# A subtraction on GpSimd exchanged for an activation and an accumulating DMA, in a kernel that splits its weights in two

## The chip, the cores and the metric

The kernel runs on one core of one Trainium2 chip. The metric is the time of one execution on the device in microseconds (us); lower is better. The engines are named as in the profile: PE is TensorE, DVE is VectorE, ACT is ScalarE, POOL is GpSimd, SP is SyncE.

## What is computed

Two transformer blocks follow each other over 256 tokens of width 1024. The first has three kinds of attention (differential, forgetting and chunked), a gated MLP with a short convolution, and a per-layer embedding. The second has two layers: an mLSTM with stick-breaking attention, then a gated delta rule, each followed by cross attention to a memory of 256 rows and by a squared-ReLU MLP. Nearly all of the arithmetic is in products with weight matrices:

```python
def reference(x, p, ln_mix, w_in, ...):
    x = first_block(x, p, ln_mix, w_in, ...)
    return second_block(x, mem_2, mix_norm_2, ab_w_in_2, ...)

def second_block(x, mem, ...):
    memn = rmsnorm(mem, mem_norm)
    for l in range(DEPTH_2):
        h = rmsnorm(x, mix_norm[l])
        if l % 2 == 0:
            x = x + ab_mixer(h, ...)
        else:
            x = x + c_mixer(h, ...)
        x = x + mem_cross_attn(rmsnorm(x, xa_norm[l]), memn, ...)
        x = x + sq_relu_mlp(rmsnorm(x, mlp_norm[l]), mlp_w1[l], mlp_w2[l])
    return rmsnorm(x, final_norm)
```

All tensors are float32.

## The kernel before, in words

The weights lie in HBM as one array `w` of 188 chunks, each 128 partitions by 2048 floats (1 MB), in the order in which they are used. TensorE is fed with fp32r operands, and the accuracy of float32 is kept by splitting each operand x in two: `hi` is x rounded to fp32r, `lo` is the rest, x - hi. A product is then three matmuls (hi by hi, hi by lo, lo by hi), so a chunk costs PE 48 matmuls of 256 columns.

`fetch` (line 436) loads and splits a chunk. It takes two halves of 1024 columns one after the other. For each, a DMA on SP's queue brings the half into a tile `raw` (line 448, four buffers), ACT writes `hi` as a rounded copy of it (line 452), and a tensor_tensor writes `lo` = raw - hi (line 454). That subtraction runs on DVE for most halves. The table `W["pool"]` (line 21) says for each chunk whether POOL does the second half (1), both (2) or none (0); there are 67 such halves, the two first of them of 512 columns (the very first chunk is loaded in quarters), the others of 1024. The names `lo`, `hi` and `raw` in the rows are these tiles. `hi` and `lo` have three buffers each.

`chunk` (line 463) is called when PE's program comes to a chunk; it makes sure that this chunk and the two after it have been fetched. The new chunk's `hi` and `lo` therefore wait for the matmuls of the chunk three before, and PE needs them two chunks later. `gemm_ab` (line 470) and `gemm_c` (line 498) issue the 48 matmuls of a chunk; in `gemm_ab` the second half is first read in the middle of the chunk, in `gemm_c` at its fourth matmul, unless it is called with `mid`.

Between the matmuls `pump` lets the other tasks issue their steps: the attentions, the convolutions and the delta rule. PE's instructions stay in the order of the program. On DVE, ACT, POOL and SP the order is laid down when the program is built, by a scheduler that plays the program through on a clock of its own; each engine then runs its list strictly in that order, and an instruction that waits holds up all behind it. So the change can move instructions which it does not name.

The stage from 803 to 964 us is `c_mixer` (the delta rule). Here DVE runs convolutions in float32 (tiles `Vm`, six scalar_tensor_tensor per chunk, line 375), products with decays (`X`), and a serial solve of small triangular blocks in `base` (tiles `t` and `I`, lines 1554 and 1556) whose result goes through HBM (`di`, `ci`) to the `solve` steps. At the start of the program (0 to 20 us) `norm` makes the first operand while chunk 0 is loaded in quarters; the statistics `R` and `rc` are written by ACT (`rstd`, line 555), and ACT's `V` needs `rc`.

Of the kernel before, what the change touches and what calls it, by code (L numbers as in the profile page):

```python
# [8 lines left out]
F32 = mybir.dt.float32  # L9
F32R = mybir.dt.float32r  # L10
AF = mybir.ActivationFunctionType
ALU = mybir.AluOpType
# [252 lines left out]
class Prog:  # L265
# [170 lines left out]
    def fetch(self, i, between=None):  # L436

        if i in self.cache or i >= len(CH):
            return
        hi = self.ring.tile([128, 2048], F32R, tag="hi", name="hi")  # L440
        lo = self.ring.tile([128, 2048], F32R, tag="lo", name="lo")
        for n in range(2):
            raw = self.ring.tile([128, 1024], F32, tag="raw", name="raw", bufs=4)
            for q in range(2 if between else 1):
                w = 512 if between else 1024
                s = slice(1024 * n + w * q, 1024 * n + w * q + w)
                r = raw[:, w * q:w * q + w]
                self.lastload = self.nc.sync.dma_start(r, self.io["w"][i, :, s]).ins.name
                if between:
                    between(2 * n + q)  # L450
                pl = n >= 2 - W["pool"][min(i, len(W["pool"]) - 1)]
                a = self.act(hi[:, s], r, AF.Copy)
                self.lastcast = a.ins.name
                d = self.tt(lo[:, s], r, hi[:, s].bitcast(F32), ALU.subtract, self.nc.gpsimd if pl else None)
                if self.after:
                    self.order(a, self.after[0])
                    if not pl:
                        self.order(d, self.after[1])
        self.after = None
        k = 8 if CH[i][2] == "A" else 2  # L460
        self.cache[i] = hi.rearrange("p (k c) -> p k c", k=k), lo.rearrange("p (k c) -> p k c", k=k)
# [1313 lines left out]
```

## Time and profile before

| | us |
|---|---|
| median of three runs | 1338.04 |
| lowest and highest of them | 1329.89, 1340.52 |
| the profiled execution | 1327.06 |
| its span, first to last instruction | 1325.3 |

The profile is of one execution, a little below the lowest of the three runs. In it PE is busy for 95% of the span, DVE for 70%, ACT for 55% and POOL for 21%; the mean granted clock of PE is 0.986. In the rows, "busy" is the time in which an engine had an instruction in execution, and the bracket behind a row is the time for which its engine was idle before it and what ended that wait.

### The profile page before, as it was taken

To read this page: it belongs to the slowest core of one execution; us is meant where nothing else is said; L and a number is where in the kernel's file an instruction comes from. 1 tells how busy PE (TensorE), PEld (TensorE's weight loads), DVE (VectorE), ACT (ScalarE), POOL (GpSimd) and SP (SyncE) were. 2 spreads that over 40 slices of the span, in tenths; PEclk is the share of its full clock that TensorE was granted. 3 is DMA by queue.
4 is the path that set the end of the run, shared out by engine and by line. 5 is a ranking of instruction groups with operands and counts; after the bars stand their busy time and mean duration, and the time that the engine had idled before them with its cause. 6 is when DMAs were issued, how large, how long until landed. Compare 5 with 4: busy or idle time off the path is not lost. (4 is left out here: it accounts for less than half of the span.)

```text
span 1325.3 us, 24944 instructions
## 1 busy us (share of the span) xinstructions
PE 1261.3 (95%) x10195; PEld 1220.8 (92%) x10195; DVE 922.0 (70%) x1401; ACT 727.8 (55%) x1217; POOL 276.1 (21%) x160
## 2 busy tenths in 40 slices
PE   8899999999999999989999999888899989999997
PEld 8788889999999999989999998878799989999997
DVE  6777678777887664786656657988685385865564
ACT  6665475655486554655444446554553564644442
POOL 4500330000224200262000015434204271100000
PEclk8999989999999999999999999999999999999999
DMA  8433455555566544444655555433334343456551
GB/s 271 137 106 106 140 163 178 177 190 192 176 212 198 186 145 144 149 136 141 206 189 182 185 184 171 134 92 119 95 108 136 111 145 128 161 189 191 187 185 43
DMA packets 65698, 208.40 MB, mean 157 GB/s; under 512 B 13192, under 2 KB 14752, under 8 KB 65584
## 3 DMA queue, kind: packets, MB, share of 16 engines
q1 hardware_dynamic: 56976, 200.76, 46.4%
q0 software_dynamic: 1600, 4.88, 1.2%
q10 hardware_dynamic: 7008, 1.18, 0.5%
q8 instruction: 80, 1.31, 0.4%
q14 instruction: 34, 0.28, 0.1%
HBM read 205.32 MB, written 1.44 MB: 156 GB/s over the span
## 5 line engine op out<-in xcount | busy, mean ns | idle before, releaser
L355 ACT ACTIVATE hi<-raw 128x1024 fp32r<-128x1024 f32 (+1 forms) x378 | 378.7, 1047 | 223.1 <-issue 98.2
L372 DVE TENSOR_TENSOR lo<-raw,hi 128x1024 fp32r<-128x1024 f32 (+1 forms) x311 | 378.5, 1251 | 164.6 <-ACT hi L355 164.1
L381 PE MATMUL pg<-oh,hi 128*128 128x256 f32 x1632 | 467.0, 286 | 7.1 <-DVE K L372 2.7
L381 PE MATMUL pg<-ol,hi 128*128 128x256 f32 x1632 | 459.3, 281 | 4.6 <-DVE ol L375 4.0
L381 PE MATMUL pg<-oh,lo 128*128 128x256 f32 x1632 | 457.5, 280 | 0.0
L381 PEld LDWEIGHTS pg<-oh,hi 128*128 128x128 f32 x1632 | 308.5, 189 | 11.9 <-issue 3.4
L381 PEld LDWEIGHTS pg<-ol,hi 128*128 128x128 f32 x1632 | 308.0, 189 | 9.9 <-DVE ol L375 8.5
L381 PEld LDWEIGHTS pg<-oh,lo 128*128 128x128 f32 x1632 | 308.7, 189 | 0.0
L372 POOL TENSOR_TENSOR lo<-raw,hi 128x1024 fp32r<-128x1024 f32 (+1 forms) x67 | 170.9, 2564 | 630.8 <-ACT hi L355 613.8
L381 PE MATMUL acc<-mh,hi 128*128 128x256 f32 x688 | 193.4, 281 | 0.7 <-ACT mh L355 0.7
L381 PE MATMUL acc<-mh,lo 128*128 128x256 f32 x688 | 193.3, 281 | 0.0
L381 PE MATMUL acc<-mlo,hi 128*128 128x256 f32 x512 | 143.9, 281 | 0.0
L381 PEld LDWEIGHTS acc<-mh,lo 128*128 128x128 f32 x688 | 131.9, 192 | 0.0
L381 PEld LDWEIGHTS acc<-mh,hi 128*128 128x128 f32 x688 | 129.2, 188 | 1.0 <-ACT mh L355 0.9
L381 PE MATMUL pg<-hi,oh 128*128 128x256 f32 x352 | 105.0, 298 | 6.2 <-DVE u L372 3.6
L381 PE MATMUL pg<-lo,oh 128*128 128x256 f32 x352 | 101.1, 287 | 1.1 <-DVE lo L372 1.1
L381 PE MATMUL pg<-hi,ol 128*128 128x256 f32 x352 | 100.8, 286 | 0.0
L381 PEld LDWEIGHTS acc<-mlo,hi 128*128 128x128 f32 x512 | 96.1, 188 | 0.0
L381 PE MATMUL acc<-oh,hi 128*128 128x256 f32 x320 | 91.8, 287 | 0.5 <-ACT oh L355 0.5
L381 PE MATMUL acc<-ol,hi 128*128 128x256 f32 x320 | 90.5, 283 | 0.0
L381 PE MATMUL acc<-oh,lo 128*128 128x256 f32 x320 | 90.2, 282 | 0.0
L372 POOL TENSOR_TENSOR sq<-sq 128x512 f32<-128x512 f32 (+1 forms) x20 | 27.5, 1375 | 255.9 <-ACT sq L355 254.6
(382 smaller groups left out, 1917.0 us busy)
## 6 DMA issues: line engine op xcount, KB each, us to landing
raw<-in_w SPq DMA_DIRECT2D x374, 512.0 KB, 4.4
mt<-in_memT POOLq DMA_DIRECT2D x12, 256.0 KB, 3.7
h<-in_xT SPq DMA_DIRECT2D x4, 256.0 KB, 4.6
raw<-in_w SPq DMA_DIRECT2D x4, 256.0 KB, 5.1
fl<-in_rel SPq DMA_DIRECT2D x3, 256.0 KB, 5.8
gw<-in_gw POOLq DMA_DIRECT2D x2, 256.0 KB, 3.2
out<-h SPq DMA_DIRECT2D x2, 256.0 KB, 2.7
con<-in_con SPq DMA_DIRECT2D x1, 384.0 KB, 8.2
```

Source lines behind the costliest of these rows:

```text
L355: return self.nc.scalar.activation(out, in_, func, **k)
L372: return (eng or self.nc.vector).tensor_tensor(out, a, b, op)
L381: i = self.nc.tensor.matmul(out, lhsT=l, rhs=r, start=start, stop=stop, skip_group_check=True)
```

## The change

For the halves that the table gives to POOL, ACT writes the negated copy of `raw` into `lo`, rounded like `hi`, right behind the copy into `hi`; then a DMA issued by POOL reads the same half of the weights from HBM once more and adds it onto `lo`. In the end `lo` is again w - hi. The table is unchanged, and so are the other halves.

```diff
                 pl = n >= 2 - W["pool"][min(i, len(W["pool"]) - 1)]
                 a = self.act(hi[:, s], r, AF.Copy)
                 self.lastcast = a.ins.name
-                d = self.tt(lo[:, s], r, hi[:, s].bitcast(F32), ALU.subtract, self.nc.gpsimd if pl else None)
+                if pl:
+
+                    self.act(lo[:, s], r, AF.Copy, scale=-1.0)
+                    self.nc.gpsimd.dma_start(lo[:, s], self.io["w"][i, :, s], accum_op=ALU.add)
+                else:
+                    d = self.tt(lo[:, s], r, hi[:, s].bitcast(F32), ALU.subtract)
                 if self.after:
```

PE's list is the same, instruction for instruction. The others differ as follows, besides the exchange itself.

ACT at the start, before. `R` and `rc` are the statistics of the first norm, `hi` of 1024 columns belong to chunks 1 and 2, `con`, `blkr` and `gwp` are constants and gate weights:

```order
L355 ACTIVATE hi<-raw 128x512
L355 ACTIVATE sq<-h 128x512 x2
L355 ACTIVATE hi<-raw 128x1024 x2
L359 ACTIVATE R<-ps_278,eps 128x256
L359 ACTIVATE rc<-ps_278,eps 128x2
L355 ACTIVATE hi<-raw 128x1024
L359 ACTIVATE R<-R 128x256
L359 ACTIVATE rc<-rc 128x2
L355 ACTIVATE hi<-raw 128x1024
L355 ACTIVATE blkr<-con_182 128x128
L355 ACTIVATE V<-pg,rc 128x256 x2
```

The same place now:

```order
L355 ACTIVATE hi<-raw 128x512
L355 ACTIVATE lo<-raw 128x512
L355 ACTIVATE sq<-h 128x512 x2
L355 ACTIVATE hi<-raw 128x1024 x4
L355 ACTIVATE blkr<-con_184 128x128
L355 ACTIVATE gwp<-gw 128x8x64
L355 ACTIVATE con_198<-raw 128x512
L359 ACTIVATE R<-ps_280,eps 128x256
L359 ACTIVATE rc<-ps_280,eps 128x2
L355 ACTIVATE hi<-raw 128x1024
L359 ACTIVATE R<-R 128x256
L359 ACTIVATE rc<-rc 128x2
```

The negated copy came in behind `hi`, and `R` and `rc` moved behind the casts of `gwp` and `con`, for whose DMAs ACT waits.

ACT in the middle of `c_mixer`, before, at about 894 to 911 us of the profile (`K` and `u` are steps of the convolution, `ssq` small evictions):

```order
L355 ACTIVATE hi<-raw 128x1024 x2
L355 ACTIVATE ssq<-ps_10394 128x4
L359 ACTIVATE K<-Vm 128x512
L355 ACTIVATE u<-K 128x512
L355 ACTIVATE Vm<-u,cols 128x256 x2
L355 ACTIVATE hi<-raw 128x1024 x2
L355 ACTIVATE ssq<-ps_10472 128x4
L359 ACTIVATE K<-Vm 128x512
```

The same place now:

```order
L355 ACTIVATE hi<-raw 128x1024 x2
L355 ACTIVATE lo<-raw 128x1024
L355 ACTIVATE Vm<-u,cols 128x256 x2
L355 ACTIVATE ssq<-ps_10438 128x4
L359 ACTIVATE K<-Vm 128x512
L355 ACTIVATE hi<-raw 128x1024 x2
L355 ACTIVATE u<-K 128x512
L355 ACTIVATE lo<-raw 128x1024 x2
L355 ACTIVATE Vm<-u,cols 128x256 x2
```

One or two negated copies stand in front of each pair of `Vm`, and `u` now follows a pair of `hi`.

POOL in the second layer's mixer, before:

```order
L372 TENSOR_TENSOR sq<-sq 128x512 x2
L372 TENSOR_TENSOR u<-sq 128x256
L517 DMA gw<-in_gw 128x512
L1046 DMA mt<-in_memT 128x512 x2
L372 TENSOR_TENSOR lo<-raw,hi 128x1024 x2
L1046 DMA mt<-in_memT 128x512
L372 TENSOR_TENSOR lo<-raw,hi 128x1024 x19
L1046 DMA mt<-in_memT 128x512
```

And now:

```order
L372 TENSOR_TENSOR sq<-sq 128x512
L457 DMA lo<-in_w 128x1024
L372 TENSOR_TENSOR sq<-sq 128x512
L372 TENSOR_TENSOR u<-sq 128x256
L522 DMA gw<-in_gw 128x512
L1051 DMA mt<-in_memT 128x512 x2
L457 DMA lo<-in_w 128x1024
L1051 DMA mt<-in_memT 128x512
L457 DMA lo<-in_w 128x1024 x19
L1051 DMA mt<-in_memT 128x512
```

From here to the end of the stage POOL computes nothing; it only issues DMAs.

## Rows read from the trace of the kernel before

**Rows 1.** The page's first part: busy time of each engine.

```profile
PE 1261.3 (95%) x10195; PEld 1220.8 (92%) x10195; DVE 922.0 (70%) x1401; ACT 727.8 (55%) x1217; POOL 276.1 (21%) x160
```

**Rows 2.** Busy time by stage: stage, its length, engines (instructions), clock, DMA share, GB/s.

```profile
0.00:62.00 62.00, 52.09 (x365) 48.62 (x365) 47.54 (x91) 41.51 (x77) 33.72 (x27) 0.94 0.64 210
...
200.00:346.00 146.00, 144.71 (x1225) 144.34 (x1225) 114.36 (x179) 83.60 (x127) 0.00 (x0) 1.00 0.56 185
...
803.00:860.00 57.00, 50.32 (x391) 47.75 (x389) 50.84 (x69) 35.79 (x60) 30.68 (x16) 0.97 0.47 149
860.00:964.00 104.00, 88.58 (x626) 78.16 (x625) 83.91 (x170) 59.26 (x118) 31.96 (x12) 0.97 0.33 100
...
1062.00:1140.00 78.00, 71.87 (x581) 69.11 (x580) 58.76 (x74) 45.86 (x82) 32.99 (x19) 1.00 0.39 125
```

**Rows 3.** The same, instructions on tile lo alone: PE, PEld, DVE, POOL.

```profile
803.00:860.00 57.00, 31.38 (x110) 21.19 (x109) 7.11 (x5) 24.83 (x9) 0.97 0.47 149
860.00:964.00 104.00, 37.39 (x130) 25.73 (x130) 7.20 (x6) 31.96 (x12) 0.97 0.33 100
```

**Rows 4.** The page's costliest groups: ACT's hi and POOL's lo.

```profile
L355 ACT ACTIVATE hi<-raw 128x1024 fp32r<-128x1024 f32 (+1 forms) x378 | 378.7, 1047 | 223.1 <-issue 98.2
...
L372 POOL TENSOR_TENSOR lo<-raw,hi 128x1024 fp32r<-128x1024 f32 (+1 forms) x67 | 170.9, 2564 | 630.8 <-ACT hi L355 613.8
```

**Rows 5.** Timeline of DVE, 895 to 920 us: start, duration, instruction.

```profile
897.14 0.18 DVE L372 TENSOR_TENSOR t<-I,N 64x25 f32<-64x25 f32 x1
897.25 0.47 DVE L375 SCALAR_TENSOR_TENSOR Vm<-u,cols,Vm 128x253 f32<-128x253 f32 x1
```

**Rows 6.** Timeline of POOL in the same stretch.

```profile
903.08 6.00 POOL L372 TENSOR_TENSOR lo<-raw,hi 128x1024 fp32r<-128x1024 f32 x2 [3.09 <-ACT hi L355]
912.15 5.08 POOL L372 TENSOR_TENSOR lo<-raw,hi 128x1024 fp32r<-128x1024 f32 x2 [3.07 <-ACT hi L355]
```

**Rows 7.** The chain that ended last, 885 to 920 us: start, share, what.

```profile
897.83 2.21 DVE t L372
...
912.57 4.94 DVE Vm L375 x2
```

**Rows 8.** Timeline around chunk 113 (w2 of layer 0): ACT, then PE.

```profile
751.19 2.01 ACT L355 ACTIVATE hi<-raw 128x1024 fp32r<-128x1024 f32 x2 [3.65 <-issue]
753.10 0.58 ACT L355 ACTIVATE r<-pg 128x512 f32<-128x512 f32 x1
...
762.95 0.28 PE L381 MATMUL acc<-mh,lo 128*128 128x256 f32 x1
```

**Rows 9.** DMA queues and issues (KB each, us to landing); POOL's issuing time by line.

```profile
q1 hardware_dynamic: 56976, 200.76, 46.4%
...
raw<-in_w SPq DMA_DIRECT2D x374, 512.0 KB, 4.4
mt<-in_memT POOLq DMA_DIRECT2D x12, 256.0 KB, 3.7
...
con<-in_con SPq DMA_DIRECT2D x1, 384.0 KB, 8.2
...
L1046 POOL DMA_DIRECT2D mt<-in_memT x12 | 6.5, 546 | 27.5 <-DVE ol L375 22.9 <-DVE u L372 3.2 <-DVE oh L372 0.8
```

**Rows 10.** Timeline of ACT and POOL at the start, 3 to 48 us.

```profile
11.71 0.63 ACT L355 ACTIVATE hi<-raw 128x512 fp32r<-128x512 f32 x1 [1.05 <-DMA raw<-in_w]
...
18.80 0.48 ACT L359 ACTIVATE R<-ps,eps 128x256 f32<-128x256 f32 x1 [2.94 <-DVE lo L372]
...
23.05 0.64 ACT L355 ACTIVATE con<-raw 128x512 fp32r<-128x512 f32 x1
...
12.42 1.42 POOL L372 TENSOR_TENSOR lo<-raw,hi 128x512 fp32r<-128x512 f32 x1 [1.19 <-ACT hi L355]
```

**Rows 11.** Timeline of DVE and PE, 57 to 63 us.

```profile
58.49 3.39 DVE L375 SCALAR_TENSOR_TENSOR E<-E,s 128x128 f32<-128x128 f32 x2
...
62.53 0.80 PE L381 MATMUL ps<-w,blkr 128*128 128x512 f32 x1 [4.77 <-DVE w L372]
```

## The prediction, made before the changed kernel was run

> **What bounds the kernel now.** I began with the busy times [rows 1]: PE is in execution for 1261.3 of 1325.3 us, so whatever the other engines do, at most 64 us of pauses can be won, and only where PE pauses. The table by stage [rows 2] shows where. In the MLP from 200 to 346 us PE rests 1.3 us in 146: work on DVE, ACT or POOL is free there as long as it is in time. From 803 to 860 us PE rests 57 - 50.3 = 6.7 us, from 860 to 964 us 15.4, from 0 to 62 us 9.9, from 1062 to 1140 us 6.1; the other 26 us lie scattered. In the two stages of `c_mixer` DVE is the fullest after PE: 50.8 of 57 us (89%) and 83.9 of 104 (81%), against 63% and 57% for ACT.
>
> Much of that DVE time is no work. On a quiet DVE a `t` product takes 0.18 us and a `Vm` step 0.47 us [rows 5]. On the chain that ended last, a `t` takes 2.21 us and two `Vm` take 4.94 us [rows 7]; POOL is just then subtracting a `lo`, in the second case from 912.15 to 917.23 us [rows 6]. A DVE instruction that starts beside POOL's subtraction stands until POOL is through. That is 2.21 - 0.18 = 2.0 us for one half and (4.94 - 0.94) / 2 = 2.0 us for each of the others, close to the 2.56 us that a subtraction lasts [rows 4]. Between 895 and 920 us POOL subtracts five halves, and the chain shows four such pieces, of which the first and the last stand in the rows: some 10 us of the chain are POOL's doing.
>
> **The change, part by part.**
>
> *67 subtractions leave POOL.* Their 170.9 us [rows 4] cost nothing in themselves; what they cost is DVE's stalls, and of those only what reaches PE. Stage by stage: 860 to 964 us has 12 of the halves [rows 3]; five of them hold the chain for 10 us, and PE has 15.4 us to give back. Behind the stalls the next thing is the serial `t`/`I` solve itself and its way through HBM, which stay. I take 10. From 803 to 860 us there are 9 halves, 18 us of stalls at the same price, but only 6.7 us of pauses, and ACT rises there from 35.8 us by 9 x 1.05 to 45.2 of 57; I take 3. From 0 to 62 us a pair of short `E` steps lasts 3.39 us, and PE then waits 4.77 us for what DVE does next [rows 11]. Some 2.5 us of this go, and as much for the half before it; ACT's two copies in front of an eviction take some back: 3. From 1062 to 1140 us, where POOL goes on subtracting `kk` and `vv` and so still stalls DVE, 2 of 6.1. All other stages together: 4. Sum: 22 us.
>
> *67 copies come to ACT.* The nearest row is its own rounding copy of the same shape, 1047 ns [rows 4]: 65 x 1.05 and two of half the size, 69 us, ACT from 728 to 797 us (60%). They stand directly in front of evictions and activations that DVE or PE await. They are hidden where ACT waits for DVE anyway; at their worst they cost 69 us, at best nothing. In the MLP stages PE needs nothing sooner than before, so a microsecond of ACT is free. In `c_mixer` the copies fall into waits which DVE's stalls made, and these shrink together. I have already counted that against the 3 us of the stage 803 to 860, and add 2 us for everything else.
>
> *67 DMAs come to POOL's queue.* Issuing costs POOL 0.55 us by its own DMAs [rows 9], in place of 2.56, so what is queued behind on POOL comes earlier, once ACT's copy is done. No accumulating DMA is in this trace. From below its landing is bounded by the 3.7 us of half the size from the same queue, from above by the slowest load here, 8.2 us for 384 KB, scaled to 512 KB: 10.9. The nearest row is the plain load of the same 512 KB, 4.4 us; as it must read its destination too, I take 6. It adds 34.6 MB of reads: a load of 0.52 MB holds 16 DMA engines for 0.464 x 1325 / 200.76 x 0.52 = 1.6 us [rows 9], 67 of them 8% of the span, twice that if the destination counts like a source. From a share of 0.33 to 0.47 in `c_mixer` [rows 2] there is room for it.
>
> Is 6 us in time? In a stage where PE never pauses, chunk 113 is the measure [rows 8]: ACT ends `hi` at 753.20 and `r` at 753.68 us, the negated copy would end at 754.73, and PE reads the half at 762.95. So 8.2 us remain. At 6 us it is hidden by PE's work on the two chunks before; every microsecond over 8.2 stops PE by as much, in about 12 chunks (those of POOL's that lie where PE does not pause).
>
> The Trainium skill ("Collectives: The Full Stack", "The bandwidth ceiling: the fold count and why AG ≠ RS ≠ AR") says that a reduce in the DMA path is slower not for its addition but because it reads two sources through one ring, at about half the rate of a copy. No run here shows it; as an estimate from it the landing would be 4.4 + 1.6 = 6.0 us, and the sum stays as it is.
>
> *The first chunk.* Here nothing lies in front as cover. POOL ends its second quarter at 13.84 us [rows 10]. Now ACT's `hi` ends at 12.34, the negated copy of 512 columns at 12.9 to 13.0, and a DMA of 256 KB lands 3.7 us after its issue [rows 9], at 16.7: 3 us later, with PE waiting, since this `lo` ends the first chunk. In the new order ACT's `R` also stands behind the cast of `con`, which ran at 23.05 us where `R` ran at 18.80 [rows 10], so that the `V` behind it comes some 4 us later and holds a PSUM bank. Both push the same PE work: 4 us in all, between 0 and 7.
>
> **Sum.** -22 + 2 + 4 = -16 us. The profiled execution took 1327.06 us (span 1325.3 and 1.8 around it) and would take 1311. The median of the runs is 1338.04, 11 us above the profile; taken from that, 1322 us, or 1.2% less. About 1% is what a measurement of this kernel tells from no change.
>
> **Rivals.**
>
> *The accumulating DMA is late (slower).* Place: the chunks with 8.2 us to spare. At the upper bound of 10.9 us, 12 chunks x 2.7 = 32 us, twice the net gain: 1338 - 16 + 32 = 1354 us. It decides from about 9.5 us on, where 12 x 1.3 is the 16 us gained. For it: nothing in the trace does this operation, and the reads go to engines that are busy half of the time. Against it: the median 4.4 us is far away. Chance 0.17.
>
> For this rival the Trainium skill has a rule too ("SBUF — State Buffer", "SBUF: two separate sides"): DMAs from GpSimd's queue have their descriptors written by its cores, and a fast-mode copy on VectorE locks them out. The 12 issues of `mt` here took 546 ns on the mean and landed in 3.7 us, which shows no such wait; the rule alone would lengthen landings by less than a microsecond beside DVE's short steps.
>
> *ACT takes DVE's place (no change).* The copies stand in the same alternation of DVE and ACT that the stalls stretched. If a quarter of the 69 us of copies lies on it, 17 us, instead of the 2 that I count, the gain is gone: 1338 - 22 + 17 + 4 = 1337 us. For it: ACT would fill 45 of 57 us from 803 to 860. Against it: around 895 to 920 us ACT waits for DVE, not the reverse. Chance 0.29.
>
> *All of DVE's stalls come back.* If PE wins 80% of its 38 us of pauses in the four stages named and the start costs nothing: 30 us, 1308. Against it: `kk`, `vv` and the way through HBM remain. Chance 0.08.
>
> **How the numbers follow.** The forecast has the remaining 0.46; its own range, gains of 8 to 24 us, is 1314 to 1330. The range for the time reaches from 1302, just below the third rival, to 1352, almost the whole of the first. Faster by over 1% (below 1325): the third rival and most of the forecast, 0.08 + 0.39 = 0.47. Slower by over 1% (above 1351): the first rival and a little of the second, where ACT costs more than its price above, 0.17 + 0.03 = 0.20. Within 1%: 0.33.
>
> **What would show it.** In the profile after: POOL busy for some 140 us, 67 issues on L457 of about 0.55 us, landing near 6 us; DVE busy for some 60 to 70 us less, no `t` or `Vm` of over 1 us from 860 to 920 us; ACT at 797 us; PE's pauses from 860 to 964 us down from 15 to about 5 us; the end of chunk 0 about 3 us later. I am wrong if PE waits for `lo` from a DMA in the MLP stages, if landings lie above 9 us, or if DVE idles behind ACT's `lo` in `c_mixer` for as long as it stood behind POOL.

## The result, and the profile after

The changed kernel takes 1365.8 us (median of 4 runs, 1363.6 to 1373.5) against 1336.9 us before (now of 4 runs, too): a ratio of 1.024, 95% interval 1.021 to 1.028. It is slower by 29 us; the forecast was 1322 us and the range ended at 1352. The profiled execution took 1366.05 us, its span 1364.2.

The page's first part, its DMA queues, the group of POOL's issues and the landings (line, KB each, median us), of the changed kernel:

```profile
PE 1279.9 (94%) x10195; PEld 1240.9 (91%) x10195; DVE 847.0 (62%) x1401; ACT 789.5 (58%) x1284; POOL 158.5 (12%) x160
...
q1 hardware_dynamic: 56976, 200.76, 45.0%
q0 software_dynamic: 11248, 39.48, 14.5%
...
L457 POOL DMA_DIRECT2D lo<-in_w x67 | 58.3, 878 | 744.2 <-ACT lo L355 538.5
...
raw<-in_w SPq DMA_DIRECT2D x374, 512.0 KB, 4.8
lo<-in_w POOLq DMA_DIRECT2D x65, 512.0 KB, 9.8
...
lo<-in_w POOLq DMA_DIRECT2D x2, 256.0 KB, 7.4
```

Beside [rows 1], DVE is busy 75 us less and ACT 62 us more, about as announced. What was not announced stands in the last rows: an accumulating DMA keeps POOL for 0.88 us and lands 9.8 us after its issue, where the sum had taken 0.55 and 6. Nor was it announced that PE is busy 18.6 us longer for the same 10195 matmuls: of the 38.9 us between the two spans (1364.2 and 1325.3) only 20.3 are pauses of PE. The other half is its clock, which was granted at 0.964 on the mean, against 0.986. Busy time by stage, columns as in [rows 2]:

```profile
0.00:62.00 62.00, 51.16 (x357) 47.86 (x358) 41.37 (x91) 46.46 (x83) 24.03 (x27) 0.94 0.74 233
200.00:346.00 146.00, 144.72 (x1226) 144.30 (x1225) 114.51 (x177) 84.59 (x129) 0.14 (x1) 1.00 0.56 183
803.00:860.00 57.00, 48.67 (x376) 47.60 (x377) 31.18 (x57) 38.68 (x61) 10.90 (x13) 0.92 0.73 204
860.00:964.00 104.00, 87.57 (x611) 81.44 (x611) 61.58 (x157) 66.01 (x110) 11.97 (x14) 0.88 0.74 178
1062.00:1140.00 78.00, 66.90 (x517) 65.16 (x516) 37.41 (x61) 51.59 (x98) 23.85 (x20) 0.91 0.64 168
```

From 860 to 964 us DVE has 22 us less to do than in [rows 2], and yet PE rests 104 - 87.6 = 16.4 us there, as before 15.4, and at a granted clock of 0.88 instead of 0.97. The DMA engines, which before carried a share of 0.33, are at 0.74. How a wait costs clock as well is seen around the late `lo` of chunk 117, in the same columns:

```profile
785.00:798.00 13.00, 13.00 (x113) 13.00 (x112) 4.44 (x5) 6.91 (x8) 1.73 (x2) 1.00 0.70 185
798.00:805.00 7.00, 1.97 (x9) 1.48 (x8) 4.29 (x7) 3.19 (x5) 0.00 (x0) 0.69 1.04 323
805.00:815.00 10.00, 10.00 (x80) 10.00 (x79) 2.79 (x4) 2.31 (x3) 0.00 (x0) 0.88 0.20 63
```

PE works without a pause at full clock, rests 5 us of 7, and then works without a pause again, but part of that stretch at the lower of its two levels (1.2 in place of 2.4 GHz): a mean of 0.88. PE's waits in the trace of after (us in total, times, longest us); the first and the third are new, and the second, with 8.3 us in one piece beside the solve's way through HBM, had been 4.9 us in four pieces:

```profile
PE acc L381 <- DMA lo<-in_w: 14.2, 6, 3.2
PE pg L381 <- DVE u L372: 12.8, 2, 8.3
PE pg L381 <- DMA lo<-in_w: 5.9, 1, 5.9
```

The chain that ended last, the pieces of it that are DMAs of `lo` or of the solve's first way through HBM (start, length, what), with one `t` of the solve among them:

```profile
10.31 7.24 DMA lo<-in_w
...
611.22 12.90 DMA lo<-in_w
766.94 8.91 DMA lo<-in_w
791.53 12.87 DMA lo<-in_w
...
903.16 7.86 DMA N<-dn
...
911.05 0.15 DVE t L372
...
927.49 7.28 DMA di<-I
...
934.79 8.99 DMA ci<-di
...
1081.22 12.96 DMA lo<-in_w
```

Read from the top: the first `lo` of the program; chunk 87, where both halves go to POOL's queue and the second lands 12.9 us after its issue; chunk 113, a single one, 8.9 us; chunks 117 and 147, pairs again. These are also all the chunks in which PE waits for a `lo` of a DMA. Between them stand three small transfers of 64 KB, the solve's way through HBM (`N`, `di`, `ci`), with 7 to 9 us each. The `t` that took 2.21 us in [rows 7] takes 0.15, and no `t` or `Vm` of the delta rule takes over 1 us any more. So the stalls are gone, and two kinds of DMA waits stand in their place. The experiments separate the two and price what was won.

### The profile page after: what moved, and what is told of

Its sections match the earlier page's. It is cut to its first block, busy times and chain, and to the rows that moved or that the text cites. A ratio compares the mean times of both kernels' runs of the same rounds, so it can differ in the third digit from the quotient of the medians.

```text
span 1364.2 us, 25027 instructions
## 1 busy us (share of the span) xinstructions
PE 1279.9 (94%) x10195; PEld 1240.9 (91%) x10195; DVE 847.0 (62%) x1401; ACT 789.5 (58%) x1284; POOL 158.5 (12%) x160
## 3 DMA queue, kind: packets, MB, share of 16 engines
q0 software_dynamic: 11248, 39.48, 14.5%
## 4 chain that ended last, share of the span: by engine, by line
PE 71%; DMA 10%; ACT 7%; DVE 7%; issue 3%; POOL 1%; SPq 0%; DVEq 0%; ACTq 0%; POOLq 0%
PE pg L381 40%; PE acc L381 28%; DMA lo<-in_w 4%; PE ps L381 2%; ACT hi L355 2%; DMA raw<-in_w 2%; DVE ol L375 2%; DVE lo L372 2%; ACT lo L355 1%; DMA ci<-di 1%; DMA di<-I 1%; DVE h L372 1%; PE acc L393 1%; DMA gw<-in_gw 1%; DMA N<-dn 1%
## 5 line engine op out<-in xcount | busy, mean ns | idle before, releaser
L381 PEld LDWEIGHTS pg<-ol,hi 128*128 128x128 f32 x1632 | 311.4, 191 | 7.2 <-DVE ol L375 5.7
L457 POOL DMA_DIRECT2D lo<-in_w x67 | 58.3, 878 | 744.2 <-ACT lo L355 538.5
L381 PEld LDWEIGHTS pg<-hi,oh 128*128 128x128 f32 x352 | 70.4, 200 | 17.4 <-DVE u L372 13.2
```

What stands on the lines that cost most here:

```text
L381: i = self.nc.tensor.matmul(out, lhsT=l, rhs=r, start=start, stop=stop, skip_group_check=True)
L457: self.nc.gpsimd.dma_start(lo[:, s], self.io["w"][i, :, s], accum_op=ALU.add)
```

## The experiments

Every run was timed against the kernel before on the same chip; so the ratios can be compared with each other, and one point (0.01) is 13.4 us.

| run | what it is | ratio to before | median us |
|---|---|---|---|
| changed kernel | | 1.024 (1.021 to 1.028) | 1365.8 |
| e1 | no DMA, copy alone | 0.989 (0.986 to 0.992) | 1318.8 |
| e2 | plain DMA | 1.000 (0.999 to 1.002) | 1335.7 |
| e3 | all on DVE | 0.982 (0.979 to 0.984) | 1310.1 |
| e4 | DMA where there is slack, POOL elsewhere | 1.004 (1.002 to 1.006) | 1340.1 |
| e5 | DMA in tight chunks alone | 1.012 (1.008 to 1.016) | 1351.8 |
| e6 | DMA in the others alone | 1.001 (1.000 to 1.003) | 1336.9 |
| e10 | e6 without eleven around the solve | 0.987 (0.983 to 0.991) | 1319.1 |
| e7 | copy and POOL's subtraction | 1.033 (1.031 to 1.034) | 1379.1 |
| e14 | copy twice, no DMA | 1.013 (1.010 to 1.016) | 1349.9 |
| e8 | e3, with nine of the DMAs | 0.985 (0.983 to 0.987) | 1315.9 |
| e9 | e3, and POOL's other work on DVE | 0.987 (0.985 to 0.989) | 1319.5 |
| e11 | copy ahead of the rounding | 1.019 (1.016 to 1.022) | 1363.7 |

**Is it the DMA, or ACT?** The diff of e1 against the changed kernel:

```diff
                     self.act(lo[:, s], r, AF.Copy, scale=-1.0)
-                    self.nc.gpsimd.dma_start(lo[:, s], self.io["w"][i, :, s], accum_op=ALU.add)
```

> The changed kernel with ACT's negated copy, but without the accumulating DMA: the addition of the weights is left out, so the lo of these 67 halves is the negated rounded weight, and PE, DVE and ACT do exactly the work of the changed kernel. Theory A (the loss is the DMA: it lands in 9.8 us on the median and in 12.9 us as the second of a pair, and it slows the other DMAs of c_mixer): all of the 29 us of loss goes, and the gain from DVE's stalls shows, 1310 to 1325 us; PE waits for no lo from a DMA, and the chunks (cg,0) and (cg,1) start no later than before. Rival B (the copies of ACT, or the new order on ACT, are the loss): 1350 us or more. Rival C (half and half, the stalls were worth nothing): 1333 to 1342 us, as before.

Measured: 1318.8 us, 3.5 points or 47 us under the changed kernel. PE waits for no `lo` from a DMA. Theory A stands: all of the loss, and more, is the DMA's. What is left without it is a gain of 1.1 points, 15 us. The page's first part of e1:

```profile
PE 1253.6 (96%) x10195; PEld 1215.2 (93%) x10195; DVE 847.6 (65%) x1401; ACT 787.8 (60%) x1284; POOL 102.2 (8%) x93
```

The work of DVE and ACT is that of the changed kernel. The order is not quite: some 35 of ACT's 1284 instructions and 47 of DVE's 1401 stand elsewhere, so the 47 us hold what that does, too. The next run does not have this flaw: in e2 both engines run the changed kernel's order, instruction for instruction.

**Is it the accumulation, or any transfer from POOL's queue?** e2:

```diff
-                    self.nc.gpsimd.dma_start(lo[:, s], self.io["w"][i, :, s], accum_op=ALU.add)
+                    self.nc.gpsimd.dma_start(lo[:, s], self.io["w"][i, :, s])
```

> The changed kernel with a plain DMA from POOL's queue in place of the accumulating one: the same 67 transfers from HBM to the same places, after the same copies, but the sum is left out (lo becomes the rounded weight itself). It prices the accumulation against the traffic and the queue. Theory A1 (the second source that an accumulation reads is what makes it late): landing 5 to 7 us, no late lo in the tight chunks, 1315 to 1335 us. Rival A2 (POOL's queue and its descriptors are what is slow, whatever the operation): landing again near 9.8 us and 12.9 us as second of a pair, 1355 to 1370 us. Between them, in proportion to the landing.

Measured: 1335.7 us, just over the end of A1's range. The page of e2, queue, issues and landings:

```profile
q0 software_dynamic: 11248, 39.48, 8.6%
...
L457 POOL DMA_DIRECT2D lo<-in_w x67 | 36.2, 540 | 741.0 <-ACT lo L355 540.9
...
lo<-in_w POOLq DMA_DIRECT2D x65, 512.0 KB, 6.4
```

The same packets and bytes, and without the addition 0.54 us to issue and 6.4 us to land. The accumulation adds 0.34 and 3.4 us. In the tight chunks 6.4 us is in time: of PE's waits for `lo` 5.4 us remain, 5.0 of them in the first chunk. So of the 47 us, 32 go with the accumulation (1.024 against 1.000), and 15 come with plain traffic as well. The solve's way through HBM is slow here too, on the chain of e2:

```profile
899.59 5.54 DMA di<-I
905.15 7.30 DMA ci<-di
```

**Late `lo`, or traffic in c_mixer?** e5 and e6 split the 67 issues by the time from the issue to PE's first read in the changed kernel's trace, under 13 us and over it:

```diff
+                    if i in (0, 16, 17, 49, 50, 51, 52, 60, 62, 64, 81, 86, 87, 113, 117, 121, 130, 140, 142, 147):
-                    self.nc.gpsimd.dma_start(lo[:, s], ...
+                        self.nc.gpsimd.dma_start(lo[:, s], ...
```

(e6 has `not in`.)

> The changed kernel with the accumulating DMA kept only in the chunks where its trace shows less than 13 us from the issue to PE's first use (30 of the 67 issues: chunks 0, 16, 17, 49 to 52, 60, 62, 64, 81, 86, 87, 113, 117, 121, 130, 140, 142, 147); in the others the addition is left out and ACT's negated copy stands alone. With its counterpart, which keeps the other 37, and the run that keeps none (1318.75 us), it splits the 47 us that the DMAs cost. Theory A-late (PE waits for lo that lands 9 to 13 us after its issue; by the steps in the chunk starts of the changed kernel about 30 us: 5 at the start, 6 at chunk 87, 8 at 113 and 117, 7 at 147, 4 elsewhere): 1343 to 1355 us. Rival A-contention (what matters is the DMAs in c_mixer beside the solve's round trip): 1322 to 1332 us.

> The counterpart: the accumulating DMA kept only in the 37 halves that PE reads 13 us or more after the issue, the addition left out in the other 30, where ACT's negated copy stands alone. No lo is late then. Theory A-late: these cost only what they take from other DMAs, about 15 us by the steps at (cqk2,2), (cg,0) and (cg,1) in the changed kernel: 1328 to 1338 us, with the round trip's di and ci again at 7 to 9 us on the chain. Rival A-contention: 1343 us or more. Rival (37 late enough cost nothing): 1316 to 1323 us. If the two parts add up, this and its counterpart together exceed the copy-only run by 47 us.

Measured: e5 1351.8 us, 2.25 points or 30 us over e1; e6 1336.9 us, 1.2 points or 16 us over e1. Together 46 us of the 47: the two parts add up. Both ranges of theory A-late held. In e5 PE's waits for `lo` are nearly those of the changed kernel:

```profile
PE acc L381 <- DMA lo<-in_w: 12.9, 6, 3.2
PE pg L381 <- DMA lo<-in_w: 6.9, 2, 6.2
```

That is 20 us of waiting, 6.2 of them in the first chunk and the rest in chunks 87, 113, 117, 142 and 147. The other 10 us are likely to be clock: for the same matmuls PE is busy 1270.3 us here and 1253.6 in e1, at a mean granted clock of 0.974 against 0.990. (The profile of e1 is of the fastest of its four runs, so 16.7 us is more than the medians hold; no run here has the waits without the clock.) In e6 PE waits 1.3 us for `lo` in all, and its 16 us must come from elsewhere. e10 takes from e6 the eleven issues of chunks 127, 128, 129 and 132 to 134, which fall beside the solve:

> The run that keeps the addition only where there is slack (37 issues, 1336.93 us), without the eleven issues of chunks 127, 128, 129 and 132 to 134, which fall around the solve's round trip through HBM from 870 to 935 us; the addition is left out there too, so 26 issues remain. Theory A-contention (these DMAs and the trip's small ones, N, di and ci, run into each other): 1322 to 1328 us, N, di and ci of the first trip at 2 to 5 us as without any DMA, and no step at (cg,1). Rival (the cost lies in all 37 alike, 0.5 us each): 1330 to 1334 us.

Measured: 1319.1 us, the same as with no DMA at all (0.987 against 0.989), somewhat under the range. All of the 16 us hangs on these eleven issues, and the other 26 cost nothing that can be measured: DVE and ACT run the very order of e1 in e10, and the two intervals nearly coincide. The landings of `ci` (its legs of the way through HBM, shortest, median, longest), in e6 and then in e10:

```profile
DMA to landing us min/median/max: 4.5/6.5/9.4
```

```profile
DMA to landing us min/median/max: 2.1/2.3/4.1
```

The chain of e6 at that place has one leg of 9.45 us, that of e10 one of 2.58 us and no `ci`:

```profile
917.37 9.45 DMA ci<-di
```

```profile
899.54 2.58 DMA di<-I
```

In the first of the two ways through HBM the traces have `N` at 4.7 us in e6 and 4.8 in e10, `di` at 7.2 and 2.6, `ci` at 9.5 and 2.2: 12 us longer for `di` and `ci` together, and the serial chain waits for both. Counted by the same matmul in both traces, PE falls 15 us further behind e10 at this one place (from 909 to 916 us of e10); the order of a few of DVE's and ACT's instructions differs there as well, so not all of the 15 need be the two transfers. It does not take an accumulation: the plain DMAs of e2 made `di` 5.5 and `ci` 7.3 us long, and e2 is 15 us over e1, 5 of them PE's wait in the first chunk. e4 had asked the same with a complete kernel: the DMA from chunk 122 to 153 where there is slack, POOL's subtraction elsewhere. (Its text counts 37 of 39; the kernel issues 30 of the 37 in that stretch.)

```diff
+                if pl and 122 <= i <= 153 and i not in (130, 140, 142, 147):
...
+                    d = self.tt(lo[:, s], r, hi[:, s].bitcast(F32), ALU.subtract, self.nc.gpsimd if pl else None)
```

> The accumulating DMA only where the changed kernel's trace shows 13 us or more from its issue to PE's first use: 37 of the 39 halves of POOL's from chunk 122 to 153, but chunks 130, 140, 142 and 147; all other halves are subtracted by POOL as before. Theory A-tight (most of the loss is lo that is late in tight chunks): 1320 to 1335 us, no later than before. Rival A-contention (most of it is that these DMAs slow the round trip of the solve through HBM, dn, di and ci, in c_mixer): 1345 to 1360 us, with the steps of 7 and 4 us at (cg,0) and (cg,1) still there.

Measured: 1340.1 us, on neither side: the tight chunks are cured (PE waits 2.9 us for `lo` in all), which leaves c_mixer. There the chain has the same two legs as in the changed kernel:

```profile
909.94 8.13 DMA di<-I
918.09 8.98 DMA ci<-di
```

**What did the freed DVE win, and what did ACT's copies cost?** e7 keeps the copy and lets POOL subtract over it:

```diff
-                    self.nc.gpsimd.dma_start(lo[:, s], self.io["w"][i, :, s], accum_op=ALU.add)
+                    self.tt(lo[:, s], r, hi[:, s].bitcast(F32), ALU.subtract, self.nc.gpsimd)
```

> ACT's negated copy stays, and POOL subtracts over it as in the kernel before, in place of the accumulating DMA: so the copies of the changed kernel with the subtractions of the kernel before. Against the copy-only run it gives the price of POOL's subtraction alone, against the kernel before the price of ACT's copies alone. Theory (POOL's subtraction holds DVE up, at about 16 to 24 us of PE's time; copies cost 0 to 10 us): 1335 to 1348 us, with t and Vm steps of over 2 us again between 860 and 920 us. Rival (the gain of the copy-only run came from the lighter order on DVE and POOL, not from POOL's hold): within 5 us of the copy-only run's 1318.75 us.

Measured: 1379.1 us, the slowest of all and far over the theory's range. POOL's subtraction costs 4.4 points, 58 us, over e1; the copies cost 3.3 points, 44 us, over the kernel before. A place that shows how the two add up is `cc`, a convolution, which passes from ACT to DVE and back. ACT, then DVE, of e7 (start, length, instruction):

```profile
367.93 1.04 ACT L355 ACTIVATE lo<-raw 128x1024 fp32r<-128x1024 f32 x1
368.88 1.08 ACT L355 ACTIVATE cc<-u,cols 128x256 f32<-128x256 f32 x2
...
372.57 0.42 ACT L359 ACTIVATE sl<-cc 128x256 f32<-128x256 f32 x1 [2.31 <-DVE cc L375]
```

```profile
369.49 2.99 DVE L375 SCALAR_TENSOR_TENSOR cc<-u,cols,cc 128x255 f32<-128x255 f32 x3 [1.16 <-ACT cc L355]
```

The same DVE steps in e1, and then, at such a place, in the kernel before:

```profile
351.83 1.37 DVE L375 SCALAR_TENSOR_TENSOR cc<-u,cols,cc 128x255 f32<-128x255 f32 x3 [1.16 <-ACT cc L355]
```

```profile
354.31 3.53 DVE L375 SCALAR_TENSOR_TENSOR cc<-u,cols,cc 128x255 f32<-128x255 f32 x4 [0.21 <-ACT cc L355]
```

ACT's copy stands in front of its own `cc`, and DVE waits 1.16 us for that where it waited 0.21 without a copy (there it does four steps in a row, beside POOL as well); then its three steps take 2.99 us beside POOL, 1.37 without. Copy and hold (the time for which DVE stands beside POOL) lie one behind the other on the same alternation of ACT and DVE. The same is seen in `c_mixer`: DVE's waits for ACT's `Vm` (us in total, times, longest), in the kernel before from 803 to 964 us and in e1 over the same matmuls, from 796 to 949 us:

```profile
DVE Vm L375 <- ACT Vm L355: 3.6, 5, 1.2
```

```profile
DVE Vm L375 <- ACT Vm L355: 14.2, 9, 3.4
```

That leaves the price of the copies where nobody holds DVE; e14 makes the copy a second time, in place of the DMA:

```diff
-                    self.nc.gpsimd.dma_start(lo[:, s], self.io["w"][i, :, s], accum_op=ALU.add)
+                    self.act(lo[:, s], r, AF.Copy, scale=-1.0)
```

> As the copy-only run, with ACT's negated copy made twice in a row for each of the 67 halves: 70 us more of ACT, no DMA, nothing on POOL; the addition of the weights is left out. It prices ACT's copies where POOL does not hold DVE. Behind POOL's subtractions they cost 43 us (1379.13 against the 1336 us of before). Theory P (the price as the prediction put it: without the hold they fall into waits, and a few us reach PE): 1320 to 1328 us. Rival (0.6 us of each copy lies on the alternation of ACT and DVE, hold or not): 1355 us or more.

Measured: 1349.9 us, 2.4 points or 32 us over e1. Neither range holds it, but it is nearer to the rival's: 0.48 us of time for each copy. Not all of that is PE waiting; between the two profiles PE's pauses grow by 15 us (54 to 69) and its busy time by 25 (1253.6 to 1278.4), at a mean granted clock of 0.971 against 0.990. (The second copy mostly stands behind the next eviction and not, as its text says, directly behind the first.) If the first 67 cost as much as these, freeing DVE was worth 15 + 32 = 47 us; in e7 it was worth 58.

**Is there something better?** e3 sets `pl = False`, so that DVE does all 378 subtractions:

> All 67 halves subtracted on DVE, as the other 311 are: neither POOL, nor ACT's negated copy, nor a DMA. DVE's own subtraction stands in the trace of before with 1221 ns at the median. It bounds from the other side what POOL's subtraction costs: DVE loses 1.2 us a half instead of standing some 2.0 us beside POOL, but in order and in front of what it does next. Theory A (a POOL subtraction costs DVE more than DVE's own would): not slower than before, 1320 to 1338 us. Rival (the stalls mostly fell where DVE could stand, and DVE's own work does not): 1345 us or more.

Measured: 1310.1 us, 1.8 points under the kernel before and the fastest of all, faster than the theory's range. The page's first part of e3:

```profile
PE 1264.6 (96%) x10195; PEld 1225.1 (93%) x10195; DVE 916.1 (70%) x1468; ACT 728.1 (55%) x1217; POOL 101.6 (8%) x93
```

DVE does 67 instructions more and is busy for 6 us less than in [rows 1]: without any of the 67 halves DVE is busy for 847.6 us (e1), so its own subtractions of them weigh 69 us, and what it had stood beside POOL 74.

e8 is e3 with `pl = pl and 122 <= i <= 128`:

> DVE subtracts all halves but the nine of chunks 122 to 128 that were POOL's in the two stages where DVE is fullest; these nine keep ACT's copy and the accumulating DMA, and are read 15 us or more after the issue. Against the run with all halves on DVE (1310.12 us) it tells whether the change is worth something where it has slack. Theory (nine subtractions of 1.2 us fewer on a DVE that bounds there, nine late enough DMAs that nobody waits for): 1302 to 1309 us. Rival (ACT's copies and the slower DMAs of the round trip take it back): 1310 to 1318 us.

Measured: 1315.9 us. Nine of the DMAs, each with slack, make e3 slower by 0.35 points, at the edge of what the intervals tell apart; they bring nothing. The rival's reading fits, though which of its two causes it is stays open.

e9 also takes from POOL its other element-wise work (`tt` and `ts` ignore the engine that they are given):

> As the run with all halves on DVE, and POOL's other subtractions, products and sums (kk, vv, w, sq, u, dbias; 60 of them, POOL busy for 90 us) go to DVE too, so that POOL only issues DMAs. Theory (any element-wise work on POOL holds DVE up for longer than DVE would need for it: 60 times 0.7 us on DVE against stalls that stood in the trace of before with 34 to 40 us): no worse than 1310.12 us, 1298 to 1310 us. Rival (where DVE is the fuller engine, its own work costs more than the hold): 1314 us or more.

Measured: 1319.5 us, slower than e3 by 0.5 points, with intervals that just part. (By the first parts of the two profiles 66 of POOL's instructions went, 93 to 27; its text counts 60.) The rival's figure holds: here POOL's short operations are better left where they are. Why stays open.

**Would an earlier issue help?** e11 moves the copy and the DMA ahead of the rounding copy:

```diff
+                if pl:
+                    self.act(lo[:, s], r, AF.Copy, scale=-1.0)
+                    self.nc.gpsimd.dma_start(lo[:, s], self.io["w"][i, :, s], accum_op=ALU.add)
                 a = self.act(hi[:, s], r, AF.Copy)
```

> The changed kernel, complete, with ACT's negated copy ahead of the rounding copy instead of behind it, so that each accumulating DMA is issued about 1 us sooner after the weights land, while hi of that half is 1 us later. Theory A-late (every microsecond over what PE leaves counts, in some 12 tight chunks): 8 to 14 us less than the changed kernel, 1352 to 1358 us. Rival (the landing is set by what else the DMA engines carry, or the contention is all): no difference, 1362 to 1369 us.

Measured: 1363.7 us (1.019 against 1.024, intervals that overlap), in the rival's range. It tells little, since the scheduler left ACT's order nearly as it was: 22 of 1284 instructions stand elsewhere. ACT at chunk 113, of e11:

```profile
760.74 2.01 ACT L355 ACTIVATE hi<-raw 128x1024 fp32r<-128x1024 f32 x2 [3.65 <-issue]
762.66 0.58 ACT L355 ACTIVATE r<-pg 128x512 f32<-128x512 f32 x1
763.13 1.05 ACT L355 ACTIVATE lo<-raw 128x1024 fp32r<-128x1024 f32 x1
```

Still `hi`, `hi`, `r`, `lo`, and the median landing is again 9.7 us. A fourth buffer for `lo`, which would let the DMA start before PE has done with the chunk three before, was not tried.

## Why the prediction was wrong, step by step

- **The failing step is "I take 6" for the landing, and with it the DMA's price of nothing in the sum.** The landing measured 9.8 us on the median, 8.9 for the single one at chunk 113 and 12.9 for the second of a pair at chunks 87, 117 and 147; the DMA's price measured 47 us (e1). The bounds 3.7 to 10.9 held the median, but not those second ones, since no part of the sum counts two transfers in a row on one queue. I chose the row nearest in size, `raw`, which comes by SP's queue. A plain transfer from POOL's queue takes 6.4 beside the traffic that the change brings (e2), so the base was 2 us off before the second source was counted. From there on it goes as the text says, and PE stops for what lands late, but in four chunks and not in twelve.
- **The rival "The accumulating DMA is late" named what happened**, with a chance of 0.17, and its point of 9.5 us lies just under the measured 9.8. That its price of 32 us is close to the 30 of e5 is luck: it stands for 12 chunks with 2.7 us each, where the trace of the changed kernel has 14.2 us of waits in four chunks, 13 of them in the three with pairs; the rest of the 30 is the first chunk, which the sum counted apart, and clock.
- **"There is room for it" failed in `c_mixer`.** The share became 0.74, and the question was not whether there is room for these transfers but what the small ones beside them wait: 16 us by the eleven DMAs beside the solve (e6, e10), which neither the sum nor a rival had.
- **No term had the clock.** The text prices a late `lo` with "every microsecond over 8.2 stops PE by as much". Half of the 38.9 us between the two profiles is PE working at a lower granted clock (0.964 against 0.986), not PE waiting.
- **"22 us" from DVE's stalls: the mechanism was right, the size was not.** `t` steps at 0.15 us, DVE busy 75 us less. It was worth 47 to 58 us (e14, e7), more than twice the term. I had priced only the stalls that the chain shows in four stages. In e7 PE falls behind e1 in some twenty steps of 1 to 7 us all along the program, counted every 48 matmuls.
- **"+2" for ACT's copies: wrong.** They cost 32 us without POOL's hold (e14, if the first set costs what the second does) and 44 with it (e7), inside my bounds of 0 and 69, but far from the value taken. That "in `c_mixer` the copies fall into waits which DVE's stalls made" is refuted by DVE's waits for `Vm` there, 3.6 us before and 14.2 in e1, and `cc` shows the same outside of it. The rival "ACT takes DVE's place" had the right reason, and its 17 us was still too little.
- **-22 + 2 was right by luck.** Without the DMA the change gains 15 us (e1) where the sum, without the start, has 20. Two terms too small, by 25 to 42 us each (e14, e7) and with opposite signs, cancelled.
- **The first chunk: right.** +4 was forecast (0 to 7); PE comes to chunk 1 4.8 us later in the changed kernel, 4.0 in e2, 0.6 earlier in e1. PE's one wait of 5.9 us for the first `lo` covers that, so the landing is enough to explain it. What the move of `R` and `rc` adds is not shown: in e1 they do not stand behind `con`.
- **Traffic: right in size.** I had said 8% of the span, twice that if the destination counts like a source: q0 went from 1.2% to 14.5%, and to 8.6% without the addition (e2).
- **The issue: 0.88 us, not 0.55**, which delays the second of a pair by another third of a microsecond; a small part of the error.

Of the signs named beforehand, "PE waits for `lo` from a DMA" and "landings above 9 us" both came. The third, DVE idle in `c_mixer` behind ACT, came by half: its waits for ACT's `Vm` grew by 11 us (3.6 to 14.2), while the `t` and `Vm` that had stood beside POOL had taken 23 us more than they take alone. PE's pauses from 860 to 964 us, forecast at 5, stayed at 16.

For the rule cited there ("Collectives: The Full Stack", "The bandwidth ceiling: the fold count and why AG ≠ RS ≠ AR", in the Trainium skill), which the page states of a collective's reduce, this case now has numbers for a DMA that accumulates into SBUF. Queue 0 held the DMA engines for 14.5% of 1364.2 us with the addition and 8.6% of 1331.7 without, 15.9 us (1.2% of 1325.3) being other transfers in both: 182 against 99 us for the same bytes, a factor of 1.8. So the trace agrees with about half the rate; whether the addition itself costs something it does not tell. Of the 3.8 us that the estimate of 6.0 lacks, 2.0 are its base (4.4 us of SP's queue, where POOL's has 6.4) and 1.8 the second source (3.4 us where it had 1.6).

## What to carry to other kernels

Where an added transfer has a deadline, price it with the same queue and kind of DMA, count two in a row on one queue as one behind the other, and look for small transfers on the critical chain that it will run beside: eleven DMAs that nobody was waiting for cost 16 us in this way. Where work is taken from one engine of an alternating pair and given to the other, price both sides by an experiment, since both can lie on the same chain, as they do here: the copy on ACT gave back most of what the freed DVE won. And before looking for a third engine, ask what the held engine would need for the work itself: DVE doing all the subtractions was the fastest kernel here, at 1310 us.

## What was not expected of the hardware

- An accumulating DMA of 512 KB from POOL's queue costs 0.88 us to issue and 9.8 us to land, a plain one to the same places 0.54 and 6.4; the second of two that are issued 0.9 us apart landed after 12.9 us at chunks 87 and 117.
- Small DMAs of 64 KB on ACT's queue, at 2 to 5 us without the eleven large ones beside them (e10), took up to 9.4 us beside accumulating ones (e6) and up to 7.4 beside plain ones (e2), although these were on another queue. In the kernel before, beside the loads of the weights alone, they took up to 6.6.
- DVE is busy for 916 us with 378 subtractions of its own and none on POOL (e3), and for 922 with 311 of its own and 67 on POOL.
- PE's clock fell at its waits: 5 us of rest in 7 at chunk 117 were followed by 10 us of work without a pause at a mean granted clock of 0.88, and by the mean clocks PE ran at the lower level for some 98 us in the changed kernel, 37 in the kernel before.
